# A fixed order from the output projection on, and the first down tile moved into the first pool

## The chip, the cores and the metric

The kernel runs on one core of one Trainium2 chip. The metric is device time in microseconds (us), the median of several executions; the profile shows one further execution in detail. Five engines work side by side, each on its own queue and in the order of that queue: TensorE (PE; its weight loads are shown apart as PEld), VectorE (DVE), ScalarE (ACT), GpSimd (POOL) and SyncE (SP), which here issues all loads and stores. Engines wait for each other through semaphores.

## The reference

One decoder layer on 256 tokens of width 2048, in float32:

```
h   = RMSNorm(x);  p = h @ W_in
A   = sliding-window attention on one part of p;  R = gated linear recurrence on the rest
m   = concat[RMSNorm(A), R] @ W_out
x   = x + RMSNorm_post(m)
x   = x + RMSNorm_post2( relu(RMSNorm_pre2(x) @ W_up)^2 @ W_down )
```

W_out is 2048 x 2048, W_up 2048 x 8192, W_down 8192 x 2048. The change lies between the last quarter of `@ W_out` and the first quarter of `@ W_down`.

## The kernel before, in words

Every float32 product is made of three fast products. A weight tile of 128 x 4 x 512 (1 MB) is loaded raw; ScalarE casts it to a rounded high part (`whi`), VectorE subtracts that from the raw tile to get the low part (`wlo`), and activations are split in the same way. TensorE then multiplies high by high, high activation by low weight, and low activation by high weight, adding all three in one PSUM bank (`three`, lines 109 to 113, for the steps here; `product`, line 785, later on).

Tokens come in two blocks of 128 (`tb` 0 and 1). The output projection runs in four column blocks of 512; the last one goes block by block of tokens, so that the work after it can begin on tb 0. That work is: scale by the post norm and add to x (`residual`), sum the squares of the new x (`norm2`), scale by the second norm (`hn`), and turn the result by transposes on TensorE into `h2T` (`turn`: four transposes into a PSUM bank of the tag `sc`, a copy by ScalarE for the high part, a subtraction by VectorE for the low part). The first two column blocks of W_up are made as plain products from `h2T`: block 0 one token block after the other, block 1 in alternation. After them a loop over segments covers the rest of W_up by sums of activations and weights with fewer products (the sums `s1` to `s4` are turned like `hn`), mixed with the segments of W_down. A segment is one weight tile and its matmuls; the loop prepares the tile of segment k+2 (cast and subtraction) while segment k is multiplied.

Weights live in two pools. The first, `wpool_a`, has three raw buffers and four each of `whi` and `wlo`. The second, `wpool_c`, opens after up block 1, in the same memory, with buffers X, P, Q and d (two each) and three each of `whi` and `wlo`. PSUM has three banks of the tag `sc`; a down column holds two of them from its first half to its second.

What sets the order: TensorE follows the program text from line 660 on (`order_pe`). On VectorE, ScalarE and SyncE a scheduler chooses the order until line 1013, where `order_all` fixes these too.

Of the kernel before, what the change touches and what calls it, by code (L numbers as in the profile page):

```python
# [29 lines left out]
def tile_hybrid_layer(  # L30
# [149 lines left out]
    def small(shape, tag, bufs=2):  # L180
        return cpool.tile([P] + list(shape), F32, tag=tag, name=nm(tag), bufs=bufs)
# [453 lines left out]
    def norm2(tb):  # L635
        s2 = small([4], f"s2{tb}")
        for c in range(4):
            square(x2[tb][:, c * 512:(c + 1) * 512], s2[:, c:c + 1])
        st = small([1], "st")
        nc.vector.reduce_sum(out=st, in_=s2, axis=AX.X)  # L640
        nc.vector.tensor_scalar(out=st, in0=st, scalar1=EPS, scalar2=None, op0=ALU.add)
        nc.gpsimd.tensor_tensor(out=rh[:, tb:tb + 1], in0=st, in1=mhalf[:, 0:1], op=ALU.pow)
        for c in range(4):
            cs = slice(c * 512, (c + 1) * 512)
            nc.vector.scalar_tensor_tensor(out=hn[tb][:, cs], in0=x2[tb][:, cs], scalar=rh[:, tb:tb + 1], in1=gpre[c],
                                           op0=ALU.mult, op1=ALU.mult)

    for c in range(3):
        ch = load_wide(w_out_v, 0, c * 512)
# [29 lines left out]
    def new_uT(first="mu0", second="mu1"):  # L679
        return [hpool.tile([P, 4, 2, S], F32R, tag=t, name=nm("uT")) for t in (first, second)]  # L680

    ch = load_wide(w_out_v, 0, 3 * 512, pieces=2)
    banks = [bank("pj"), bank("pj")]
    for kt in range(NKT):
        wide_step(banks[0], ch, mixT, 0, kt)
    evac_post(3, 0, banks[0])
    residual(0)
    norm2(0)
    up_w = load_wide(w_up_v, 0, 0, pieces=2)
    for kt in range(NKT):  # L690
        if kt in (9, 11, 13, 15):
            turn(0, (kt - 9) // 2)
        wide_step(banks[1], ch, mixT, 1, kt)
    evac_post(3, 1, banks[1])
    residual(1)
    norm2(1)


    uT = new_uT()
    ps = [bank("pj"), bank("pj")]  # L700
    for kt in range(NKT):
        if kt in (12, 13, 14, 15):
            turn(1, kt - 12)
        wide_step(ps[0], up_w, h2T, 0, kt)
    u = [new_u(), new_u()]
    relu(u[0], ps[0])
    for kt in range(NKT):
        if kt == 4:
            turn_u(uT, 0, 0, u[0], "tr", 1)
        wide_step(ps[1], up_w, h2T, 1, kt)  # L710
    relu(u[1], ps[1])

# [29 lines left out]
    in_h2T("a22", 1, 1)  # L742
    in_h2T("s4", 1, 0)

    up_w = load_wide(w_up_v, 0, 512)
    nc.vector.tensor_sub(out=tmp, in0=half(1, 0), in1=half(1, 1))
    nc.vector.tensor_sub(out=half(1, 0), in0=half(0, 0), in1=half(1, 0))
    ps = [bank("pj"), bank("pj")]
    for i in range(4):
        for tb in range(2):  # L750
            if i == 0 and tb == 1:
                turn_u(uT, 0, 1, u[1], "tr", 1)
            if i == 1:
                turn_sum(("s1", tmp), tb)
                if tb == 1:
                    nc.vector.tensor_sub(out=tmp, in0=tmp, in1=half(0, 0))
                    nc.vector.tensor_add(out=half(0, 0), in0=half(0, 1), in1=tmp)
            if i == 2:
                turn_sum(("s3", half(1, 0)), tb)
            if i == 3:  # L760
                turn_sum(("s2", tmp), tb)
            for j in range(4):
                wide_step(ps[tb], up_w, h2T, tb, 4 * i + j)
    prev = {}
    for tb in range(2):
        u = new_u()
        relu(u, ps[tb])
        prev[1, tb] = u

    pb.__exit__(None, None, None)  # L770
    pool_w.__exit__(None, None, None)
    wp[0] = ctx.enter_context(tc.tile_pool(name="wpool_c", bufs=2, side="right", reuse_waits="tile"))

    def raw_tile(tag, wv, kt0, c0):
        t = wp[0].tile([P, 4, 512], F32, tag=tag, name=nm(tag), bufs=2)
# [124 lines left out]
    def period(ch, m1_next):  # L900
# [40 lines left out]
        for k, to, frm, c, h in plan:  # L941
            q[k].adds.append(plus(to, frm, c, h))
        if ch == 1:
            q[0].turns += [lambda c=c: turn_sum(("s4", half(0, 0)), c) for c in range(2)]
            q[1].turns.append(t(d, 1, 0, d))
            q[2].turns.append(t(d, 1, 1, d))
            loads = [(0, "d", d, 1, 0), (1, "d", d, 1, 1), (4, "d", d, 2, 0), (7, "d", d, 2, 1),
                     (8, "R", ch, 0), (9, "R", ch, 1), (10, "d", d, 3, 0), (11, "Q", nx, 0), (12, "Q", nx, 1),
                     (13, "d", d, 3, 1), (14, "X", nx, 0), (15, "X", nx, 1), (16, "P", nx, 0), (17, "P", nx, 1),
                     (19, "d", ch, 0, 0), (21, "d", ch, 0, 1)]  # L950
# [62 lines left out]
    order_all = tc.manual_schedule(engines={mybir.EngineType.DVE, mybir.EngineType.Activation, mybir.EngineType.SP})  # L1013
    order_all.__enter__()
    load_down(0, 0, 0)
    for h in range(2):
        load_up("X", 1, h)
    load_down(0, 0, 1)
    for h in range(2):
# [53 lines left out]
```

## Time and profile before

| | us |
|---|---|
| median of 3 runs | 1118.68 (1118.08 to 1118.79) |
| the profiled execution | 1118.42 |
| its span, first to last instruction | 1116.7 |
| TensorE busy in the span | 1086.6 (97%) |
| VectorE busy | 846.1 (76%) |
| ScalarE busy | 623.1 (56%) |

The span is what the views below cut up; 1.7 us of the execution lie around it. TensorE is busy nearly always, so the views that matter are those that show where it is not: its own order in time with the idle time before each instruction and what ended it, and the clock that it was granted.

### The profile page before, as it was taken

How to read it: one execution, taken by the hardware profiler on the slowest of the kernel's cores; microseconds unless marked ns; L12 is line 12 of the kernel's file. 1: busy time of each engine (PE TensorE's matmuls, PEld its weight loads, DVE VectorE, ACT ScalarE, POOL GpSimd, SP SyncE). 2: the span in 40 equal slices, each digit the busy share in tenths (PEclk: the TensorE clock that was granted, in tenths of full speed). 3: DMA queues.
4: the chain of work that ended last, by engine and by line, in shares of the span. 5: the costliest groups of instructions: out<-in, count | busy, mean ns of one | idle time of the engine just before them, and what ended most of it. 6: DMA issues, size and time to landing. Idle time of an engine off the chain costs nothing.

```text
span 1116.7 us, 14041 instructions
## 1 busy us (share of the span) xinstructions
PE 1086.6 (97%) x5708; PEld 926.3 (83%) x5708; DVE 846.1 (76%) x765; ACT 623.1 (56%) x719; POOL 19.8 (2%) x48
## 2 busy tenths in 40 slices
PE   8999989999999989899999999999999999999996
PEld 7999889999988867778788888888888888888885
DVE  6755666665655557498998898898898898898565
ACT  6554565545454445455675575575575575575542
POOL 2100000000000000000000000000000000000000
PEclk9999989999999989999999999999999999999999
DMA  8743424444458645726728638638638638534662
GB/s 270 246 164 115 151 76 152 151 151 151 152 190 311 215 158 183 263 83 222 259 92 284 227 99 281 223 103 279 220 108 277 218 112 277 214 114 151 236 253 76
DMA packets 125538, 209.61 MB, mean 188 GB/s; under 512 B 3945, under 2 KB 49570, under 8 KB 124450
## 3 DMA queue, kind: packets, MB, share of 16 engines
q1 hardware_dynamic: 125474, 208.72, 54.7%
q8 instruction: 45, 0.74, 0.3%
q14 instruction: 19, 0.16, 0.0%
HBM read 204.51 MB, written 4.19 MB: 187 GB/s over the span
## 4 chain that ended last, share of the span: by engine, by line
PE 89%; DVE 4%; ACT 2%; issue 1%; DMA 1%; POOL 0%; DVEq 0%; POOLq 0%; ACTq 0%
PE pj L785 21%; PE pj L112 10%; PE pj L113 10%; PE pj L111 10%; PE sc L112 8%; PE sc L111 8%; PE sc L113 8%; DVE wlo L91 2%; PE o L112 1%; PE o L113 1%; PE tr L112 1%; PE tr L113 1%; PE tr L111 1%; PE o L111 1%; ACT whi L90 1%
## 5 line engine op out<-in xcount | busy, mean ns | idle before, releaser
L91 DVE TENSOR_TENSOR wlo<-raw,whi 128x2048 fp32r<-128x2048 f32 (+2 forms) x84 | 152.8, 1832 | 74.6 <-ACT whi L90 74.3
L90 ACT CAST whi<-d 128x2048 fp32r<-128x2048 f32 x60 | 114.8, 1913 | 120.5 <-PE sc L113 85.9
L91 DVE TENSOR_TENSOR wlo<-d,whi 128x2048 fp32r<-128x2048 f32 x60 | 137.4, 2290 | 55.3 <-ACT whi L90 55.2
L90 ACT CAST whi<-raw 128x2048 fp32r<-128x2048 f32 (+2 forms) x84 | 127.8, 1539 | 77.4 <-PE pj L113 38.3
L112 PE MATMUL sc<-wlo,uT 128*128 128x512 f32 x384 | 150.5, 392 | 2.5 <-DVE wlo L91 2.5
L111 PE MATMUL sc<-whi,uT 128*128 128x512 f32 x384 | 150.5, 392 | 2.2 <-ACT whi L90 1.6
L113 PE MATMUL sc<-whi,uT 128*128 128x512 f32 x384 | 150.3, 391 | 0.4 <-DVE uT L677 0.4
L90 ACT CAST whi<-X 128x2048 fp32r<-128x2048 f32 x56 | 107.1, 1915 | 77.9 <-DVE X L789 32.3
L785 PE MATMUL pj<-whi,hT 128*128 128x512 f32 x448 | 143.9, 390 | 0.0
L91 DVE TENSOR_TENSOR wlo<-X,whi 128x2048 fp32r<-128x2048 f32 x56 | 127.9, 2286 | 2.5 <-ACT whi L90 2.5
L111 PE MATMUL pj<-hT,whi 128*128 128x256 f32 x384 | 110.5, 288 | 1.1 <-ACT whi L90 0.7
L113 PE MATMUL pj<-hT,wlo 128*128 128x256 f32 x384 | 110.5, 288 | 0.9 <-DVE wlo L91 0.8
L112 PE MATMUL pj<-hT,whi 128*128 128x256 f32 x384 | 111.2, 290 | 0.0
L785 PE MATMUL pj<-whi,a 128*128 128x512 f32 x336 | 109.9, 395 | 0.0
L785 PEld LDWEIGHTS pj<-whi,hT 128*128 128x128 f32 x448 | 84.1, 188 | 17.4
L112 PEld LDWEIGHTS sc<-wlo,uT 128*128 128x128 f32 x384 | 72.5, 189 | 18.3 <-DVE wlo L91 3.4
L111 PEld LDWEIGHTS sc<-whi,uT 128*128 128x128 f32 x384 | 72.4, 189 | 18.0 <-ACT whi L90 1.8
L785 PE MATMUL pj<-wlo,hT 128*128 128x512 f32 x224 | 87.2, 390 | 0.0
L113 PEld LDWEIGHTS sc<-whi,uT 128*128 128x128 f32 x384 | 72.5, 189 | 15.8 <-DVE uT L677 0.8
L91 DVE TENSOR_TENSOR wlo<-P,whi 128x2048 fp32r<-128x2048 f32 x32 | 73.2, 2291 | 13.8 <-ACT whi L90 13.8
L111 PE MATMUL pj<-whi,hT 128*128 128x512 f32 x192 | 76.0, 398 | 0.0
L111 PEld LDWEIGHTS pj<-hT,whi 128*128 128x128 f32 x384 | 74.1, 193 | 2.0 <-ACT whi L90 0.9
(262 smaller groups left out, 2041.6 us busy)
## 6 DMA issues: line engine op xcount, KB each, us to landing
d<-in_w_down_dram SPq DMA_DIRECT2D x60, 1024.0 KB, 5.0
P<-in_w_up_dram SPq DMA_DIRECT2D x28, 1024.0 KB, 5.5
raw<-in_w_in_dram SPq DMA_DIRECT2D x24, 1024.0 KB, 5.1
raw<-in_w_in_dram SPq DMA_DIRECT2D x35, 512.0 KB, 4.6
raw<-in_w_out_dram SPq DMA_DIRECT2D x16, 1024.0 KB, 5.0
X<-in_w_up_dram SPq DMA_DIRECT2D x14, 1024.0 KB, 5.5
Q<-in_w_up_dram SPq DMA_DIRECT2D x14, 1024.0 KB, 5.4
raw<-in_w_up_dram SPq DMA_DIRECT2D x8, 1024.0 KB, 5.5
```

The costliest lines, as they stand in the source:

```text
L90: nc.scalar.copy(out=hi[:, k], in_=raw[:, k])
L91: nc.vector.tensor_tensor(out=lo[:, k], in0=raw[:, k], in1=hi[:, k].bitcast(F32), op=ALU.subtract)
L111: nc.tensor.matmul(o, lhsT=ah, rhs=bh, start=first, stop=False)
L112: nc.tensor.matmul(o, lhsT=ah, rhs=bl, start=False, stop=False)
L113: nc.tensor.matmul(o, lhsT=al, rhs=bh, start=False, stop=last)
L785: nc.tensor.matmul(o, lhsT=a, rhs=b, start=fresh and kt == 0 and i == 0, stop=kt == 7 and i == 2, skip_group_check=not fresh)
```

## The change

The fixed order now begins right after TensorE's first half of the last output column, so that VectorE, ScalarE and SyncE follow the text from there. `norm2` is gone: the squares are taken inside `residual`, right behind each quarter of x, and the scaling is split in quarters that stand among the turns. Up block 0 is no longer made step by step but in parts: for each weight tile all high-by-high products (`hh`), all with the low activation (`lh`), and last all with the low weight (`hl`), so that a low weight part is needed late. A raw tile is loaded when the third tile before it has been split (`load_t(i + 3)`), and the cast and the subtraction are written out in halves at their places. Up block 1 takes its tiles (4 to 7) from the same chain. The first tile of W_down (`raw00`, `w00`) is now loaded and split in the first pool and multiplied before the second pool opens; the segment loop then begins with the first product of `X`, and the two turns of the sum `s4`, which stood before that down tile, stand behind it. One `whi` buffer of the second pool is taken by a tile that nothing uses.

```
     def residual(tb):
         r = rsq_part(pss[tb][:, 3:4], ppart[:, tb:tb + 1])
+        s2 = small([4], f"s2{tb}")
         for c in range(4):
             cs = slice(c * 512, (c + 1) * 512)
             nc.vector.scalar_tensor_tensor(out=x2[tb][:, cs], in0=acc[tb][:, cs], scalar=r, in1=x2[tb][:, cs],
                                            op0=ALU.mult, op1=ALU.add)
+            square(x2[tb][:, cs], s2[:, c:c + 1])
...
+    def lo_t(i, h):
+        k = slice(2 * h, 2 * h + 2)
+        hi, lo = up_w[i]
+        nc.vector.tensor_tensor(out=lo[:, k], in0=up_raw[i][:, k], in1=hi[:, k].bitcast(F32), op=ALU.subtract)
+        if h == 1:
+            load_t(i + 3)
...
+    def part(tb, tile, kind):
+        for kt in range(4 * tile, 4 * tile + 4):
+            a = tok(h2T, kt, tb)[1 if kind == "lh" else 0]
+            b = up_w[tile][1 if kind == "hl" else 0][:, kt % 4, :]
+            nc.tensor.matmul(ps[tb], lhsT=a, rhs=b, start=kt == 0 and kind == "hh", stop=kt == NKT - 1 and kind == "hl")
...
-    for kt in range(NKT):
-        if kt in (9, 11, 13, 15):
-            turn(0, (kt - 9) // 2)
-        wide_step(banks[1], ch, mixT, 1, kt)
+    order_all.__enter__()
     evac_post(3, 0, banks[0])
+    residual(0)()
...
+    w3(0, 11)
+    scaled(0, 0)
+    scaled(0, 1)
+    cast2(0)
+    turn(0, 0)
+    scaled(0, 2)
+    w3(11, 13)
+    turn(0, 1)
+    cast2(1)
+    scaled(0, 3)
+    lo_t(0, 0)
+    w3(13, 15)
+    turn(0, 2)
+    w3(15, 16)
+    turn(0, 3)
     evac_post(3, 1, banks[1])
+    lo_t(0, 1)
+    cast2(2)
...
+    for tile_ in (0, 1):
+        part(0, tile_, "hh")
+    for tile_ in (0, 1):
+        part(0, tile_, "lh")
+    residual(1)()
+    part(0, 2, "hh")
+    part(0, 2, "lh")
+    cast2(3)
+    scaled(1, 0)
+    scaled(1, 1)
+    part(0, 0, "hl")
+    part(0, 3, "hh")
+    turn(1, 0)
...
+    turn(1, 3)
+    lo2(1)
+    part(1, 2, "hh")
+    part(1, 3, "hh")
+    for tile_ in range(4):
+        part(1, tile_, "lh")
+    lo2(2)
+    lo2(3)
+    part(1, 0, "hl")
+    for tile_ in range(1, 4):
+        for tb in range(2):
+            part(tb, tile_, "hl")
...
+    down_half(0, 0, 0, uT, w00, evac=False)
+    pb.__exit__(None, None, None)
+    pool_w.__exit__(None, None, None)
+    wp[0] = ctx.enter_context(tc.tile_pool(name="wpool_c", bufs=2, side="right", reuse_waits="tile"))
...
-            q = [dn[0][0], m1_first[0], m1_first[1], dn[0][1], m5[0], m5[1], dn[1][0], m6[0], m6[1], dn[1][1],
+            q = [None, m1_first[0], m1_first[1], dn[0][1], m5[0], m5[1], dn[1][0], m6[0], m6[1], dn[1][1],
...
-            q[0].turns += [lambda c=c: turn_sum(("s4", half(0, 0)), c) for c in range(2)]
+            q[1].turns += [lambda c=c: turn_sum(("s4", half(0, 0)), c) for c in range(2)]
...
+    wp[0].tile([P, 4, 512], F32R, tag="whi", name="unused", bufs=3)
     prepare(0, lambda: [load_up("Q", 1, h) for h in range(2)])
+    relu_first(0)
     prepare(1)
+    relu_first(1)
```

TensorE where the second pool opens, before: the turns of `s4` (from `hn`), then the first down tile (`whi_4344`, `wlo_4349`).

```order
L113 MATMUL pj_4167<-whi_4160,hT_3355 128x512
L627 MATMUL sc_4360<-ident,hn_3840 128x128 [waits DVE_49]
L627 MATMUL sc_4360<-ident,hn_3840 128x128 x3
L627 MATMUL sc_4367<-ident,hn_3840 128x128 [waits DVE_49]
L627 MATMUL sc_4367<-ident,hn_3840 128x128 x3
L111 MATMUL sc_4374<-whi_4344,uT_3995 128x512 [waits DVE_49,Activation_49]
L112 MATMUL sc_4374<-wlo_4349,uT_3995 128x512 [waits DVE_49]
```

The same place on TensorE now: the end of the first down tile (`whi_4271`, `wlo_4272`, banks `sc_4328` and `sc_4329`), then the turns of `s4`, then the first turn of up block 1 (`u_4381`).

```order
L112 MATMUL sc_4329<-wlo_4272,uT_3961 128x512
L113 MATMUL sc_4329<-whi_4271,uT_3961 128x512
L637 MATMUL sc_4394<-ident,hn_3857 128x128 [waits DVE_49]
L637 MATMUL sc_4394<-ident,hn_3857 128x128 x3
L637 MATMUL sc_4401<-ident,hn_3857 128x128 [waits DVE_49]
L637 MATMUL sc_4401<-ident,hn_3857 128x128 x3
L669 MATMUL sc_4408<-ident,u_4381 128x128 [waits DVE_49]
```

The down tile has moved ahead of the turns; its two banks stay taken, and the three turns behind it pass one after the other through the third bank of the tag.

VectorE at that place, before: the low parts of the first three segments, then the low parts of the turned `s4` (`hT_3352`, `hT_3353`).

```order
L91 TENSOR_TENSOR wlo_4349<-d_4332,whi_4344 128x2048 [waits DMAHW3_49,PE_49,Activation_49]
L91 TENSOR_TENSOR wlo_4353<-X_4334,whi_4352 128x2048 [waits DMAHW4_49,Activation_49]
L91 TENSOR_TENSOR wlo_4357<-X_4336,whi_4356 128x2048 [waits DMAHW5_49,Activation_49]
L630 TENSOR_TENSOR hT_3352<-sc_4360,hT_3352 128x4x128 [waits Activation_49]
L630 TENSOR_TENSOR hT_3353<-sc_4367,hT_3353 128x4x128 [waits Activation_49]
```

And now, from the low part of the first down tile (`wlo_4272`) on:

```order
L91 TENSOR_TENSOR wlo_4272<-raw_4150,whi_4271 128x2048 [waits DMAHW3_49,Activation_49]
L640 TENSOR_TENSOR a_4135<-sc_4287,a_4135 128x4x128 [waits Activation_49]
L640 TENSOR_TENSOR a_4135<-sc_4306,a_4135 128x4x128 [waits Activation_49]
L91 TENSOR_TENSOR wlo_4378<-X_4360,whi_4373 128x2048 [waits DMAHW4_49,Activation_49]
L91 TENSOR_TENSOR wlo_4384<-X_4362,whi_4383 128x2048 [waits DMAHW5_49,Activation_49]
L873 TENSOR_TENSOR X_4360<-X_4360,P_4368 128x2048 [waits DMAHW0_49,DVE_49]
L91 TENSOR_TENSOR wlo_4391<-d_4364,whi_4390 128x2048 [waits DMAHW6_49,Activation_49]
L640 TENSOR_TENSOR hT_3352<-sc_4394,hT_3352 128x4x128 [waits Activation_49]
L640 TENSOR_TENSOR hT_3353<-sc_4401,hT_3353 128x4x128 [waits Activation_49]
```

Four operations of 128 x 2048 now stand between the last low part of the first pool and the first low part of `s4`.

ScalarE at that place, before and then now: the casts of the first three segments.

```order
L90 CAST whi_4344<-d_4332 128x2048 [waits DMAHW3_49,DVE_49]
L90 CAST whi_4352<-X_4334 128x2048 [waits DMAHW4_49,DVE_49]
L90 CAST whi_4356<-X_4336 128x2048 [waits DMAHW5_49,DVE_49]
L629 CAST hT_3352<-sc_4360 128x4x128 [waits PE_49]
L629 CAST hT_3353<-sc_4367 128x4x128 [waits PE_49]
```

```order
L90 CAST whi_4373<-X_4360 128x2048 [waits DMAHW4_49,DVE_49,PE_49]
L664 ACTIVATE u_4381<-pj_4153 128x512
L90 CAST whi_4383<-X_4362 128x2048 [waits DMAHW5_49]
L664 ACTIVATE u_4387<-pj_4154 128x512
L90 CAST whi_4390<-d_4364 128x2048 [waits DMAHW6_49]
L639 CAST hT_3352<-sc_4394 128x4x128 [waits PE_49]
```

The first cast of the segment loop now has a wait for TensorE (PE_49) that it did not have before; in the built program `whi_4373` has the address of `whi_4271`, and the matmul that the wait names is the last one of the first down tile.

## Rows read from the trace of the kernel before

**Rows 1.** The page: its first line and TensorE's share.

```profile
span 1116.7 us, 14041 instructions
PE 1086.6 (97%) x5708; PEld 926.3 (83%) x5708; DVE 846.1 (76%) x765; ACT 623.1 (56%) x719; POOL 19.8 (2%) x48
```

**Rows 2.** TensorE in time: start us, us, engine, line, operation [idle before <-releaser].

```profile
402.20 0.39 PE L113 MATMUL pj<-whi,mu 128*128 128x512 f32 x1
408.13 1.12 PE L627 MATMUL sc<-ident,hn 128*128 128x128 f32 x4 [5.54 <-DVE hn L645]
...
413.83 0.60 PE L627 MATMUL sc<-ident,hn 128*128 128x128 f32 x4
...
415.65 0.60 PE L627 MATMUL sc<-ident,hn 128*128 128x128 f32 x4
...
427.24 0.63 PE L627 MATMUL sc<-ident,hn 128*128 128x128 f32 x4 [2.12 <-DVE hn L645]
...
470.95 0.50 PE L111 MATMUL sc<-whi,uT 128*128 128x512 f32 x1 [1.60 <-ACT whi L90]
473.27 0.50 PE L112 MATMUL sc<-wlo,uT 128*128 128x512 f32 x1 [1.82 <-DVE wlo L91]
...
478.28 0.50 PE L111 MATMUL sc<-whi,uT 128*128 128x512 f32 x1 [0.64 <-DVE hT L630]
...
491.25 0.50 PE L113 MATMUL sc<-whi,uT 128*128 128x512 f32 x1 [0.36 <-DVE uT L677]
...
500.19 0.50 PE L112 MATMUL sc<-wlo,uT 128*128 128x512 f32 x1 [0.66 <-DVE wlo L91]
```

**Rows 3.** The chain that ended last: start us, us, what.

```profile
505.74 5.44 PE pj L785 x24
```

**Rows 4.** Windows of 2 us: busy time of each engine, granted clock, DMA share, GB/s.

```profile
406.00:408.00 2.00, 0.00 (x0) 0.00 (x0) 1.30 (x5) 0.00 (x0) 0.55 (x1) 0.50 0.97 309
426.00:428.00 2.00, 0.76 (x6) 0.75 (x7) 1.65 (x3) 0.09 (x1) 0.31 (x1) 1.00 0.93 381
474.00:476.00 2.00, 2.00 (x7) 1.51 (x6) 2.00 (x2) 1.47 (x3) 0.00 (x0) 0.50 0.80 216
```

**Rows 5.** VectorE in time, residual and norm of token block 0.

```profile
398.70 2.74 DVE L618 SCALAR_TENSOR_TENSOR x<-mg,rf,x 128x512 f32<-128x512 f32 x4 [0.66 <-POOL rf L600]
...
404.04 2.36 DVE L91 TENSOR_TENSOR wlo<-raw,whi 128x1024 fp32r<-128x1024 f32 x2 [0.33 <-ACT whi L90]
406.32 0.15 DVE L640 TENSOR_REDUCE st<-s 128x1 f32<-128x4 f32 x1
```

**Rows 6.** ScalarE in time: the last square with its sum, and casts.

```profile
404.86 0.62 ACT L589 ACTIVATE junk<-x 128x512 f32<-128x512 f32 x1
405.39 0.18 ACT L589 ACTIVATION_READ_ACCUMULATOR junk<-x 128x1 f32 x1
...
413.34 2.00 ACT L90 CAST whi<-raw 128x1024 fp32r<-128x1024 f32 x2
...
470.79 3.70 ACT L90 CAST whi<-X 128x2048 fp32r<-128x2048 f32 x2
```

**Rows 7.** The page, DMA issues: KB each, median us from issue to landing.

```profile
raw<-in_w_up_dram SPq DMA_DIRECT2D x8, 1024.0 KB, 5.5
```

**Rows 8.** One turn in time, through TensorE, ScalarE and VectorE.

```profile
449.10 0.60 PE L627 MATMUL sc<-ident,tmp 128*128 128x128 f32 x4
...
449.73 0.59 ACT L629 CAST a<-sc 128x512 fp32r<-128x512 f32 x1 [1.95 <-PE sc L627]
...
450.35 0.69 DVE L630 TENSOR_TENSOR a<-sc,a 128x512 fp32r<-128x512 f32 x1 [0.90 <-ACT a L629]
```

**Rows 9.** VectorE in time, three operations of 128 x 2048 on end.

```profile
500.05 2.29 DVE L91 TENSOR_TENSOR wlo<-X,whi 128x2048 fp32r<-128x2048 f32 x1
502.25 2.29 DVE L789 TENSOR_TENSOR P<-P,Q 128x2048 f32<-128x2048 f32 x1
504.45 2.29 DVE L91 TENSOR_TENSOR wlo<-X,whi 128x2048 fp32r<-128x2048 f32 x1
```

More of the change, by code (lines that the diff above doesn't have):

```diff
@@ L619, in residual, with stats @@
                                            op0=ALU.mult, op1=ALU.add)
+            square(x2[tb][:, cs], s2[:, c:c + 1])
         nc.sync.dma_start(out=x2_dram[tb], in_=x2[tb])
         hn[tb] = keep.tile([P, D], F32, tag=f"acc{tb}", name=nm("hn"))
+        def stats():
+            st = small([1], "st")
+            nc.vector.reduce_sum(out=st, in_=s2, axis=AX.X)
+            nc.vector.tensor_scalar(out=st, in0=st, scalar1=EPS, scalar2=None, op0=ALU.add)
+            nc.gpsimd.tensor_tensor(out=rh[:, tb:tb + 1], in0=st, in1=mhalf[:, 0:1], op=ALU.pow)
+        return stats
     def turn_act(src, hi, lo, tag="sc", bufs=3):
@@ L633, in turn @@
         turn_act(hn[tb][:, c * 512:(c + 1) * 512], *(h2T[c][:, :, i, tb * P:(tb + 1) * P] for i in range(2)))
[L635 to L646, printed above, removed]
     for c in range(3):
@@ L680, in new_uT, with load_t, cast_t, split_t @@
         return [hpool.tile([P, 4, 2, S], F32R, tag=t, name=nm("uT")) for t in (first, second)]
+    up_raw, up_w = {}, {}
+    def load_t(i):
+        if i < 8:
+            up_raw[i] = load_raw(w_up_v[:, 4 * (i % 4):4 * (i % 4) + 4, (i // 4) * 512:(i // 4 + 1) * 512])
+    def cast_t(i, h):
+        if h == 0:
+            up_w[i] = [wp[0].tile([P, 4, 512], F32R, tag=t, name=nm(t), bufs=4) for t in ("whi", "wlo")]
+        k = slice(2 * h, 2 * h + 2)
+        nc.scalar.copy(out=up_w[i][0][:, k], in_=up_raw[i][:, k])
+    def lo_t(i, h):
+        k = slice(2 * h, 2 * h + 2)
+        hi, lo = up_w[i]
+        nc.vector.tensor_tensor(out=lo[:, k], in0=up_raw[i][:, k], in1=hi[:, k].bitcast(F32), op=ALU.subtract)
+        if h == 1:
+            load_t(i + 3)
+    def split_t(i):
+        up_w[i] = split_weight(None, up_raw[i])
+        load_t(i + 3)
+    def scaled(tb, c):
+        cs = slice(c * 512, (c + 1) * 512)
+        nc.vector.scalar_tensor_tensor(out=hn[tb][:, cs], in0=x2[tb][:, cs], scalar=rh[:, tb:tb + 1], in1=gpre[c],
+                                       op0=ALU.mult, op1=ALU.mult)
     ch = load_wide(w_out_v, 0, 3 * 512, pieces=2)
@@ L685, in tile_hybrid_layer @@
         wide_step(banks[0], ch, mixT, 0, kt)
+    for i in range(3):
+        load_t(i)
+    order_all = tc.manual_schedule(engines={mybir.EngineType.DVE, mybir.EngineType.Activation, mybir.EngineType.SP})
+    order_all.__enter__()
     evac_post(3, 0, banks[0])
-    residual(0)
-    norm2(0)
-    up_w = load_wide(w_up_v, 0, 0, pieces=2)
-    for kt in range(NKT):
-        if kt in (9, 11, 13, 15):
-            turn(0, (kt - 9) // 2)
-        wide_step(banks[1], ch, mixT, 1, kt)
+    residual(0)()
@@ new lines, in w3, with cast2 @@
+    def w3(a, b):
+        for kt in range(a, b):
+            wide_step(banks[1], ch, mixT, 1, kt)
+    ps = []
+    def part(tb, tile, kind):
[3 more added lines that the diff above has]
+            nc.tensor.matmul(ps[tb], lhsT=a, rhs=b, start=kt == 0 and kind == "hh", stop=kt == NKT - 1 and kind == "hl")
+    def cast2(i):
+        cast_t(i, 0)
+        cast_t(i, 1)
@@ L694, in tile_hybrid_layer, with lo2 @@
+    def lo2(i):
+        lo_t(i, 0)
+        lo_t(i, 1)
+    w3(0, 11)
[13 more added lines that the diff above has]
+    turn(0, 3)
     evac_post(3, 1, banks[1])
-    residual(1)
-    norm2(1)
+    lo_t(0, 1)
+    cast2(2)
     uT = new_uT()
[L700 to L704, printed above, removed]
@@ L705, in tile_hybrid_layer @@
-    u = [new_u(), new_u()]
[L706 to L711, printed above, removed]
+    ps += [bank("pj"), bank("pj")]
+    for tile_ in (0, 1):
[10 more added lines that the diff above has]
+    part(0, 3, "hh")
@@ L715, in half @@
+    turn(1, 0)
+    part(0, 3, "lh")
+    scaled(1, 2)
+    turn(1, 1)
+    part(1, 0, "hh")
+    scaled(1, 3)
+    turn(1, 2)
+    part(1, 1, "hh")
+    turn(1, 3)
[10 more added lines that the diff above has]
+            part(tb, tile_, "hl")
+    u = [new_u(), new_u()]
     def half(tb, h):
@@ L743, in tile_hybrid_layer @@
     in_h2T("s4", 1, 0)
-    up_w = load_wide(w_up_v, 0, 512)
     nc.vector.tensor_sub(out=tmp, in0=half(1, 0), in1=half(1, 1))
     nc.vector.tensor_sub(out=half(1, 0), in0=half(0, 0), in1=half(1, 0))
+    split_t(4)
+    relu(u[0], ps[0])
+    split_t(5)
+    raw00 = load_raw(w_down_v[:, 0:4, 0:512])
+    relu(u[1], ps[1])
     ps = [bank("pj"), bank("pj")]
@@ L751, in tile_hybrid_layer @@
             if i == 0 and tb == 1:
+                turn_u(uT, 0, 0, u[0], "tr", 1)
+                split_t(6)
+            if i == 2 and tb == 0:
                 turn_u(uT, 0, 1, u[1], "tr", 1)
@@ L756, in tile_hybrid_layer @@
                     nc.vector.tensor_sub(out=tmp, in0=tmp, in1=half(0, 0))
+                    split_t(7)
                     nc.vector.tensor_add(out=half(0, 0), in0=half(0, 1), in1=tmp)
@@ L761, in tile_hybrid_layer @@
                 turn_sum(("s2", tmp), tb)
+            if i == 2 and tb == 1:
+                w00 = split_weight(None, raw00)
             for j in range(4):
-                wide_step(ps[tb], up_w, h2T, tb, 4 * i + j)
+                wide_step(ps[tb], [up_w[4 + k] for k in range(i + 1)], h2T, tb, 4 * i + j)
     prev = {}
[L765 to L772, printed above, removed]
     def raw_tile(tag, wv, kt0, c0):
@@ L839, in down_half, with relu_first @@
                 evac_down(ch, c, tb, banks[tb])
+    def relu_first(tb):
+        prev[1, tb] = new_u()
+        relu(prev[1, tb], ps[tb])
+    down_half(0, 0, 0, uT, w00, evac=False)
+    pb.__exit__(None, None, None)
+    pool_w.__exit__(None, None, None)
+    wp[0] = ctx.enter_context(tc.tile_pool(name="wpool_c", bufs=2, side="right", reuse_waits="tile"))
     class Seg:
@@ L943, in period @@
         if ch == 1:
-            q[0].turns += [lambda c=c: turn_sum(("s4", half(0, 0)), c) for c in range(2)]
+            q[1].turns += [lambda c=c: turn_sum(("s4", half(0, 0)), c) for c in range(2)]
             q[1].turns.append(t(d, 1, 0, d))
             q[2].turns.append(t(d, 1, 1, d))
-            loads = [(0, "d", d, 1, 0), (1, "d", d, 1, 1), (4, "d", d, 2, 0), (7, "d", d, 2, 1),
+            loads = [(1, "d", d, 1, 1), (4, "d", d, 2, 0), (7, "d", d, 2, 1),
                      (8, "R", ch, 0), (9, "R", ch, 1), (10, "d", d, 3, 0), (11, "Q", nx, 0), (12, "Q", nx, 1),
@@ L1011, in tile_hybrid_layer @@
     segs += end + [Seg(lambda h=h: raws["d", last, 3, h], None) for h in range(2)]
[L1013 to L1017, printed above, removed]
+    load_up("X", 1, 0)
+    load_up("X", 1, 1)
     load_down(0, 0, 1)
+    load_down(0, 1, 0)
     for h in range(2):
```

## The prediction

> **What bounds the kernel now.** The page comes first. TensorE is busy for 1086.6 of 1116.7 us [rows 1], so no other engine's length matters by itself: time is won or lost only where TensorE stands or runs slowly. Next comes TensorE in time with the idle time in brackets, for the stretch that the change rewrites, 402 to 500 us. The reader is to see seven places where it loses time [rows 2]. A few corrections make the brackets into losses. In the segment loop 24 matmuls take 5.44 us, 0.227 each [rows 3], while a row shows 0.39 for one; a bracket is counted from that end, so a wait costs 0.16 more than its bracket. One turn and six matmuls take 1.82 us (413.83 to 415.65), so a turn alone takes 0.46.
>
> First place: after 402.20 TensorE is free at 402.43, waits until 408.13 for the scaled `hn`, and at 413.83 has done only two groups of turn and six matmuls, 3.64 us of work. The loss is 413.83 - 402.43 - 3.64 = 7.8 us. Of this 5.7 is the wait and 2.1 the clock: the granted clock is 0.50 of full, the level of 1.2 GHz, in the window 406 to 408 [rows 4]. Second: 2.12 + 0.16 = 2.3 at 427.24, with the clock at 1.00 there. Third and fourth, at the opening of the second pool: 1.6 for the cast, then 1.82 + 0.27 = 2.1 for the low part (the row before it has 0.50). Fifth: from 473.27 to 478.28 there are 11 matmuls, 2.5 us at the full rate, in 5.0: 2.5 lost, partly at a clock of 0.50 [rows 4]. Sixth and seventh: 0.5 and 0.8. All told 7.8 + 2.3 + 1.6 + 2.1 + 2.5 + 0.5 + 0.8 = 17.6 us. That is all that a better order can win here; the matmuls and turns themselves stay the same in number.
>
> **The change part by part.** I build up what TensorE loses in the same stretch afterwards.
>
> A, the first turn. The four updates of x still end at 398.70 + 2.74 = 401.44 [rows 5]. The last square then follows at once, since no cast stands before it: 0.71 us (404.86 to 405.57) [rows 6], to 402.2. From the sum of the squares to the turn took 408.13 - 406.32 = 1.81 [rows 2, 5], so the turn starts at 404.0. TensorE has two more steps before it than it had, six matmuls, and is free at 402.43 + 1.36 = 403.8. Loss 0.2 in place of 7.8.
>
> B, weight tile 3. Its load is queued behind the second half of tile 0's low part, which stands on VectorE behind the evacuation of the output projection. From 404.0: two groups of 1.82, then turn, three matmuls and the last turn; that turn starts at 408.8 and TensorE is free at 409.3. Copy (0.60 + 0.59 behind the turn's start) [rows 8], square 0.71, product about 0.6, half a low part 1.18 (2.36 for two) [rows 5]: 412.6. The load takes 5.5 [rows 7], half a cast 1.0 [rows 6]: 419.2. TensorE has 28 matmuls until then, 6.35 us, free at 415.6. It waits 3.5, does two matmuls, and waits another 0.5 for the second half of the cast. Loss 4.0; this takes the place of the second wait of 2.3.
>
> C, weight tile 4 for up block 1, loaded behind the low parts of tile 1. From the start of the last turn of token block 1: 1.95 for the turn through VectorE [rows 8], 2.36 for two halves, 5.5 for the load, 1.85 for the cast [rows 6], 2.29 for the low part [rows 9]: 13.95. TensorE has the turn, 52 matmuls of parts and one of block 1: 0.46 + 12.0 = 12.5. Loss 1.5.
>
> D, the opening of the second pool. The first cast of the segment loop has a new wait for the last matmul of the moved down tile, whose high part lay in that memory. Behind it on ScalarE stand the next two casts and the copy of the first `s4` turn, on VectorE everything: low part, low part, sum of X and P, low part, and only then the low part of that turn. The second `s4` turn needs the bank that this releases, as both other banks of the tag hold the down tile's results. So from the last matmul's end: cast 1.85, four operations 2.20 apart [rows 9] make 8.8, the turn's low part 0.69, handoffs about 0.15: 11.5. Add 0.16 as for every wait, take off the 0.46 of the first `s4` turn, which TensorE does meanwhile: loss 11.2. ScalarE is no later: its three casts and two short activations end before VectorE's third operation does.
>
> E, the turn behind it, again through the third bank: 1.95 from turn to low part [rows 8] less 0.46: loss 1.5.
>
> F, the clock. A wait of 5.5 us was followed by 2.1 us of slow running, and the pair of 1.60 and 1.82 by 2.5 - 0.64 - 0.16 = 1.7. Eleven microseconds are not in the trace. The bounds are 1.7 and twice 2.1, if the wait in E prolongs it; I take 2.1, as after the longest wait seen.
>
> The remaining waits of before (0.5 and 0.8) were VectorE just behind TensorE; after D, TensorE begins with the low parts of three segments ready, so they go. Sum: 0.2 + 4.0 + 1.5 + 11.2 + 1.5 + 2.1 = 20.5 against 17.6, a loss of 2.9 us.
>
> What I cost at nothing: the squares inside `residual`, the split scaling and the cast halves lie beside TensorE's matmuls but for A and B. The store of x on SyncE's queue for block 1 stands before the load of tile 4, which waits for VectorE far longer. The loads of X and d now stand behind those of tile 7 and the down tile; they are issued when tiles 4 and 5 have been split, over 20 us before D, and land in 5.5. P for the sum waits for the down tile's low part, 24 down matmuls (5.4 us) and more before D; if it were late, D would grow by as much.
>
> The profiled execution took 1118.42 us; with 2.9 it is 1121.3. The median of the runs is 0.26 above that execution, so I predict 1121.6 us.
>
> **The rivals.** First, the other side: D does not happen, because the cast need not wait for the down tile. ScalarE would be free after the last turn of up block 1, 36 matmuls (8.2 us) less a copy of about 1.2 before D begins, and everything behind it would start 7.0 earlier: D is 4.2, and the clock term perhaps 0. The time is then 1118.7 + 2.9 - 7.0 - 2.1 to 0, about 1112.5 to 1114.6. It would already be faster than before by more than can be told if D were under 6. Against it: the wait stands in ScalarE's queue in the built program, and the addresses are the same. For it: a tile is taken and not used just there, so the place in memory had some purpose.
>
> Second, the clock pays more often. The wait of 3.5 in B lies between one that did not lower the clock (2.1) and one that did (5.5); with another 2.1 there, and D's slow stretch twice as long, the loss is 2.9 + 2.1 to 2.9 + 4.2: 1123.7 to 1125.8. The Trainium skill (TensorE: Matmul & The Clock Gate, section Part 1: The HAM clock gate) says that the gate judges activity over a window that runs freely and is not started by the kernel. By that rule the wait in B would cost 2.1 in some executions and nothing in others; no row here shows a wait of that size, so the trace leaves it open.
>
> Third, no change to be told: loads land sooner and VectorE's operations start earlier than I have them, so that B is 3.0, C 0.6 and F 1.7. The loss is then 2.9 - 1.0 - 0.9 - 0.4 = 0.6: 1119.3.
>
> **How the numbers follow.** The forecast has 0.52, the second rival 0.24, the third 0.14, the first 0.10. What a measurement can tell from no change is 0.2%, 2.2 us here: above 1120.9 or below 1116.4. The forecast's own range is 1120.6 to 1123.6 (B and C half a microsecond shorter each; F at its upper bound); a tenth of it lies below 1120.9 and goes to "same". So slower 0.47 + 0.24 + 0.03 = 0.74, same 0.05 + 0.11 = 0.16, faster 0.10. The range from 1119.0 to 1125.0 leaves out the first rival and the ends of the others.
>
> **What would show it.** A: the first turn of `hn` at about 404 with almost no wait. B: a wait of 3 to 4 us before the `hh` products of tile 3, ended by the cast. C: one to two for the low part of tile 4. D: a wait of about 11 us before the second `s4` turn, ended by VectorE, with the first cast of the loop starting only when the down tile's last matmul has ended; the granted clock near 0.5 behind it. If the cast of X starts while the down tile is multiplied, D is wrong and the kernel is faster. If VectorE's queue there holds another order or the turn finds a free bank, likewise.

## The result, and the profile after

The changed kernel takes 1123.56 us (median of 5 runs, 1122.47 to 1125.39) where the kernel before takes 1118.79 in the same session: a ratio of 1.0045, 95% interval 1.0034 to 1.0057. It is slower, by about 4.8 us; 2.9 were forecast. The execution that the profile shows took 1124.23, 0.7 above the median. Its page:

```profile
span 1122.5 us, 14032 instructions
...
PE 1088.4 (97%) x5708; PEld 928.5 (83%) x5708; DVE 846.4 (75%) x765; ACT 623.0 (55%) x719; POOL 19.1 (2%) x48
```

The span is 5.8 us longer than in [rows 1]. TensorE has the same 5708 instructions, so again only its waits and its clock matter. TensorE in time, the places that answer to [rows 2]:

```profile
404.26 0.66 PE L637 MATMUL sc<-ident,hn 128*128 128x128 f32 x4 [0.18 <-DVE hn L704]
...
419.53 0.73 PE L730 MATMUL pj<-whi,hT 128*128 128x512 f32 x2 [3.46 <-ACT whi L689]
420.48 1.22 PE L730 MATMUL pj<-whi,hT 128*128 128x512 f32 x2 [0.22 <-ACT whi L689]
...
426.59 0.63 PE L637 MATMUL sc<-ident,hn 128*128 128x128 f32 x4
...
440.60 0.50 PE L112 MATMUL pj<-wlo,hT 128*128 128x512 f32 x1 [1.27 <-DVE wlo L91]
...
471.50 0.60 PE L637 MATMUL sc<-ident,hn 128*128 128x128 f32 x4
483.26 1.12 PE L637 MATMUL sc<-ident,hn 128*128 128x128 f32 x4 [11.16 <-DVE hT L640]
485.77 1.11 PE L669 MATMUL sc<-ident,u 128*128 128x128 f32 x4 [1.40 <-DVE hT L640]
...
495.02 0.39 PE L111 MATMUL sc<-whi,uT 128*128 128x512 f32 x1
```

The wait of 5.54 before the first turn has shrunk to 0.18 and that of 2.12 is gone. In their place stand 3.46 and 0.22 for the cast of weight tile 3, 1.27 for the low part of tile 4, and, between the two `s4` turns, 11.16; the turn behind them waits 1.40. (The last row is the first matmul of the next down tile; it waits for nothing.) Loads stand in the chain that ended last, just ahead of the first two of these places (start, us, what):

```profile
412.88 5.54 DMA raw<-in_w_up_dram
430.90 5.33 DMA raw<-in_w_up_dram
```

The first starts as VectorE has done the half low part that frees its buffer (411.60 + 1.22 = 412.82), and the cast starts as it has landed (412.88 + 5.54 = 418.42); VectorE's and ScalarE's rows:

```profile
411.60 1.22 DVE L694 TENSOR_TENSOR wlo<-raw,whi 128x1024 fp32r<-128x1024 f32 x1
```

```profile
418.44 1.99 ACT L689 CAST whi<-raw 128x1024 fp32r<-128x1024 f32 x2 [1.34 <-DMA raw<-in_w_up_dram]
```

Now the 11 us. ScalarE in time:

```profile
471.69 1.90 ACT L90 CAST whi<-X 128x2048 fp32r<-128x2048 f32 x1 [7.61 <-PE sc L113]
...
473.99 1.89 ACT L90 CAST whi<-X 128x2048 fp32r<-128x2048 f32 x1
...
476.26 1.90 ACT L90 CAST whi<-d 128x2048 fp32r<-128x2048 f32 x1
478.05 0.59 ACT L639 CAST hT<-sc 128x512 fp32r<-128x512 f32 x1
```

And VectorE:

```profile
473.62 4.57 DVE L91 TENSOR_TENSOR wlo<-X,whi 128x2048 fp32r<-128x2048 f32 x2 [8.82 <-ACT whi L90]
478.12 2.28 DVE L873 TENSOR_TENSOR X<-X,P 128x2048 f32<-128x2048 f32 x1
480.32 2.28 DVE L91 TENSOR_TENSOR wlo<-d,whi 128x2048 fp32r<-128x2048 f32 x1
482.52 0.68 DVE L640 TENSOR_TENSOR hT<-sc,hT 128x512 fp32r<-128x512 f32 x1
```

ScalarE stands for 7.61 us until the last matmul of the down tile (`sc`, line 113) releases its cast. VectorE has four operations on end before the one that frees the bank, and TensorE starts again 0.06 us after that one ends (482.52 + 0.68 = 483.20). The clock, in windows of 2 us (columns as in [rows 4]):

```profile
420.00:422.00 2.00, 1.78 (x7) 1.22 (x6) 0.00 (x0) 0.43 (x1) 0.00 (x0) 0.54 0.01 4
422.00:424.00 2.00, 2.00 (x9) 1.64 (x8) 0.79 (x2) 0.59 (x1) 0.00 (x0) 0.61 0.00 0
...
484.00:486.00 2.00, 0.60 (x3) 0.23 (x2) 0.69 (x1) 0.59 (x1) 0.00 (x0) 0.50 0.93 309
490.00:492.00 2.00, 2.00 (x7) 1.41 (x7) 1.10 (x1) 0.00 (x0) 0.00 (x0) 0.54 0.00 0
492.00:494.00 2.00, 2.00 (x12) 1.69 (x11) 0.04 (x1) 1.98 (x2) 0.00 (x0) 1.00 0.00 0
```

So the clock was at half, the level of 1.2 GHz, behind the wait of 3.46 too, and behind that of 11.16 until almost 492. The chain shows what this does to 12 matmuls, before and after the clock came back:

```profile
486.89 5.10 PE pj L869 x12
492.42 2.76 PE pj L869 x12
```

### The profile page after: what moved, and what is told of

The parts are those of the page before. It is cut to its first block, busy times and chain, and to the rows that moved or that the text cites. A ratio compares the mean times of both kernels' runs of the same rounds, so it can differ in the third digit from the quotient of the medians.

```text
span 1122.5 us, 14032 instructions
## 1 busy us (share of the span) xinstructions
PE 1088.4 (97%) x5708; PEld 928.5 (83%) x5708; DVE 846.4 (75%) x765; ACT 623.0 (55%) x719; POOL 19.1 (2%) x48
## 4 chain that ended last, share of the span: by engine, by line
PE 90%; DVE 3%; DMA 3%; ACT 2%; issue 1%; SPq 0%; POOL 0%; DVEq 0%; POOLq 0%; ACTq 0%
PE pj L869 22%; PE pj L112 10%; PE pj L113 10%; PE pj L111 10%; PE sc L113 8%; PE sc L111 8%; PE sc L112 8%; DVE wlo L91 2%; PE o L112 1%; PE tr L113 1%; PE o L113 1%; PE tr L112 1%; PE tr L111 1%; ACT whi L90 1%; PE o L111 1%; PE sc L669 1%
## 5 line engine op out<-in xcount | busy, mean ns | idle before, releaser
L91 DVE TENSOR_TENSOR wlo<-raw,whi 128x2048 fp32r<-128x2048 f32 (+2 forms) x77 | 145.6, 1901 | 72.5 <-ACT whi L90 71.3
L91 DVE TENSOR_TENSOR wlo<-d,whi 128x2048 fp32r<-128x2048 f32 x59 | 135.1, 2289 | 49.2 <-ACT whi L90 49.2
L90 ACT CAST whi<-raw 128x2048 fp32r<-128x2048 f32 (+2 forms) x77 | 121.8, 1596 | 80.9 <-PE pj L113 33.2
L869 PE MATMUL pj<-whi,hT 128*128 128x512 f32 x448 | 145.7, 394 | 0.0
L113 PEld LDWEIGHTS pj<-hT,wlo 128*128 128x128 f32 x384 | 74.3, 193 | 0.8 <-DVE wlo L91 0.8
```

What stands on the lines that cost most here:

```text
L90: nc.scalar.copy(out=hi[:, k], in_=raw[:, k])
L91: nc.vector.tensor_tensor(out=lo[:, k], in0=raw[:, k], in1=hi[:, k].bitcast(F32), op=ALU.subtract)
L113: nc.tensor.matmul(o, lhsT=al, rhs=bh, start=False, stop=last)
L869: nc.tensor.matmul(o, lhsT=a, rhs=b, start=fresh and kt == 0 and i == 0, stop=kt == 7 and i == 2, skip_group_check=not fresh)
```

## The experiments

Theory: the loss is made in the opening of the second pool by two things together, the memory that the first cast waits for and the one free bank that the turns pass through, and it is made larger by the clock. Rivals: the first part loses (late loads, order by parts); or the clock alone does. All ratios are to the kernel before, with 95% intervals; a time is the median of a run's executions. A recorded ratio can differ from the quotient of the medians by up to 0.13% (e_both: 1111.40 against 1118.71), so a difference of a microsecond between two runs is not certain.

| run | us | ratio to the kernel before |
|---|---|---|
| the change | 1123.56 | 1.0045 (1.0034 to 1.0057) |
| e_down_back | 1114.56 | 0.9963 (0.9950 to 0.9975) |
| e_down_only | 1125.35 | 1.0059 (1.0047 to 1.0072) |
| e_s4 | 1116.48 | 0.9983 (0.9974 to 0.9992) |
| e_buf | 1116.99 | 0.9988 (0.9979 to 0.9997) |
| e_both | 1111.40 | 0.9948 (0.9935 to 0.9962) |
| e_clock | 1121.55 | 1.0032 (1.0019 to 1.0044) |
| e_clockb | 1121.43 | 1.0026 (1.0017 to 1.0036) |
| e_parts | 1129.55 | 1.0097 (1.0081 to 1.0112) |
| e_best | 1109.10 | 0.9911 (0.9896 to 0.9926) |
| e_warm | 1107.48 | 0.9903 (0.9887 to 0.9920) |

**The two parts of the change, each alone.** First the change without the moved down tile:

```
...
-    down_half(0, 0, 0, uT, w00, evac=False)
...
-            q = [None, m1_first[0], ...
+            q = [dn[0][0], m1_first[0], ...
...
-            q[1].turns += [lambda c=c: turn_sum(("s4", ...
+            q[0].turns += [lambda c=c: turn_sum(("s4", ...
...
+    load_down(0, 0, 0)
...
```

> The changed kernel with the first down tile put back behind the opening of the second pool, as the kernel before has it (with its load, its place in the segment loop and the s4 turns ahead of it); the fixed order and the products in parts stay. This is the first part of the change alone. Theory (the first part gains, the moved down tile loses it all and more): the first turn has almost no wait, the waits of about 3.5 and 1.4 for weight tiles 3 and 4 stay, the opening of the pool shows the waits of the kernel before (1 to 3 us each, about 5 in all) and not 11: 1113.0 to 1115.5. Rival (the first part is neutral, what the first turn wins the late loads lose): 1118 to 1119.5. Rival (the first part is what loses): above 1120.

Measured 1114.56: the first part alone makes the kernel faster. TensorE at the opening of the pool:

```profile
469.21 0.50 PE L112 MATMUL sc<-wlo,uT 128*128 128x512 f32 x1 [1.11 <-DVE wlo L91]
474.23 0.50 PE L111 MATMUL sc<-whi,uT 128*128 128x512 f32 x1 [2.21 <-DVE hT L640]
```

Then the kernel before with the moved tile and nothing else:

```
+    raw00 = load_raw(w_down_v[:, 0:4, 0:512])
...
+                w00 = split_weight(None, raw00)
...
+    down_half(0, 0, 0, uT, w00, evac=False)
...
-            q = [dn[0][0], m1_first[0], ...
+            q = [None, m1_first[0], ...
...
```

> The kernel before with the moved down tile alone: loaded and split in the first pool, multiplied before the second opens, s4 turns behind it; no fixed order, no products in parts before it. This is the second part of the change alone. Theory: the waits of 5.5 and 2.1 of the kernel before stay, those at the opening of the pool (7.5 us of loss) are replaced by 11.3 + 1.6 and a half-clock stretch worth about 3.6: 7 to 9 us slower than the kernel before, 1125.5 to 1128. Rival (the two parts work only together: with the scheduler free until the pool opens, the first cast comes earlier and the wait is not there): 1118 to 1120.

Measured 1125.35, just under the range. The long wait is there to a hundredth:

```profile
486.27 1.11 PE L627 MATMUL sc<-ident,hn 128*128 128x128 f32 x4 [11.17 <-DVE hT L630]
```

So the moved tile loses and the order ahead of it gains. The two ratios make -0.37% and +0.59%, in sum +0.22%, where the change has +0.45%. That is at the edge of what the intervals allow; whether the parts hinder each other by a microsecond or two stays open.

**The two causes of the long wait.** The turns back ahead of the down tile:

```
+    for c in range(2):
+        turn_sum(("s4", half(0, 0)), c)
     down_half(0, 0, 0, uT, w00, evac=False)
...
-            q[1].turns += [lambda c=c: turn_sum(("s4", half(0, 0)), c) for c in range(2)]
```

> The changed kernel with one thing put back: the two turns of the sum s4 stand ahead of the first down tile on TensorE again. Theory (the loss lies in the opening of the second pool: the first cast waits for the down tile's memory, and the s4 turns behind the tile pass through one bank): the 11.2 us wait before the second s4 turn goes, and the 1.4 behind it; what is left is the cast and low part of the first X tile behind the down tile (1.85 + 2.2, less one turn) and the waits that the kernel before had further on (about 0.4, 2.2 and 0.9), so 5 us come back in waits and 0 to 3 in the clock: 1116.0 to 1118.7. Rival (the loss comes from the first part: loads that hang on low parts, products in parts): within 1 us of 1123.6, the 5 us turning up as other waits. Rival (the clock alone): faster by no more than the half-clock stretch behind 483 us, some 3.5 us, with the waits themselves merely moved: about 1120.

Measured 1116.48. What is left at the place is a wait of 2.48 us, now for ScalarE, where the relu stands behind the cast that still waits for the down tile:

```profile
475.34 1.12 PE L669 MATMUL sc<-ident,u 128*128 128x128 f32 x4 [2.48 <-ACT u L664]
```

The other cause by itself, the order left as it is:

```
-    wp[0].tile([P, 4, 512], F32R, tag="whi", name="unused", bufs=3)
+    unused = wp[0].tile([P, 4, 512], F32R, tag="whi", name="unused", bufs=3)
+    nc.gpsimd.memset(unused[:, 0, 0:1].bitcast(F32), 0.0)
```

> The changed kernel, in which GpSimd writes one column of the high-part tile of the second pool that nothing used, so that the tile really takes its place: the first segment's high part then lies on other memory than the moved down tile's. The order of the work is the same. Theory: the first cast of the loop no longer waits for the down tile's last matmul; the cast of the third segment, which now lies there, does. Behind the last matmul stand one cast (1.85), one low part (2.2) and the low part of the turn (0.7) instead of four operations of 2.2: the wait before the second s4 turn falls from 11.2 to about 5, the 1.4 stays, the clock gives back up to 2: 1115.5 to 1117.5. Rival (the order of the queues and not the memory makes the wait: the cast would come just as late without the dependence): 1123.6, wait still 11. Rival (first part): within 1 us of 1123.6.

Measured 1116.99. Without an access the extra tile had taken no place in memory, so the `whi` buffer that the section on the change counts as taken was still free; with one, the first two casts run beside the down tile, and only the third waits, for the write into that place, which itself comes behind the down tile's last matmul. ScalarE, then TensorE:

```profile
464.58 1.91 ACT L90 CAST whi<-X 128x2048 fp32r<-128x2048 f32 x1
...
472.47 1.90 ACT L90 CAST whi<-d 128x2048 fp32r<-128x2048 f32 x1 [3.19 <-POOL unused L1117]
```

```profile
477.35 1.11 PE L637 MATMUL sc<-ident,hn 128*128 128x128 f32 x4 [4.64 <-DVE hT L640]
```

The bank's wait falls from 11.16 to 4.64 with the same order of the queues: 6.5 of it was the memory. Both edits together:

> The changed kernel with both edits: s4 turns ahead of the down tile, and the unused high-part tile made real by a write of one column. Theory: nothing is late behind the down tile any more; both waits (11.2 and 1.4) and the half-clock stretch behind them go, and the later waits of the kernel before (about 2.2 and 0.9) come back: 9.8 us less in waits, 2 to 3.6 in the clock: 1110.2 to 1112.0, faster than the kernel before by 6 to 8. Rival (first part): not faster than the kernel before, since the late loads remain. Rival (the two edits remove the same wait twice): no better than the better of the two alone, about 1116.

Measured 1111.40. TensorE's waits between 395 and 510 us (what waits, for what: us in total, times, longest us) hold neither `s4` nor the turn behind it, but one of the kernel before's kind in the loop (`uT`, 0.36 there [rows 2] and 2.0 here), as expected:

```profile
PE pj L730 <- ACT whi L689: 3.3, 1, 3.3
PE sc L113 <- DVE uT L674: 2.0, 1, 2.0
PE pj L112 <- DVE wlo L91: 1.5, 1, 1.5
```

**The clock.** In the changed kernel, TensorE is given idle work in its long wait:

```
...
+                dead = bank("tr", 1)
+                for k in range(46):
+                    nc.tensor.matmul(dead, lhsT=uT[0][:, 0, 0, 0:P], rhs=uT[0][:, k % 4]..., start=True, stop=True)
...
```

> The changed kernel, with 46 matmuls of 128 x 512 that nothing uses on TensorE between the two s4 turns, in a bank that is free there: TensorE works through the long wait instead of standing. 46 x 0.227 = 10.4 us, so the wait falls to about 0.8 without ending later. Theory (the clock is part of the loss: it is granted at half until about 491.9, and the 7.2 us of work between 483.3 and then would take 3.6): granted clock 1.00 throughout there, 1119.5 to 1121.0, though TensorE does 10 us more work. Rival (the wait alone is the loss, the clock term was the 2.1 of the forecast or less): 1121.5 or more. Rival (the extra matmuls slow VectorE or ScalarE by their traffic): 1123.6 or more.

Measured 1121.55, outside the theory's range and just inside that of the rival by which the clock costs no more than the forecast's 2.1: 2.0 us less than the change by the medians, though the intervals of the two ratios overlap. TensorE:

```profile
472.35 10.71 PE L1040 MATMUL tr<-uT 128*128 128x512 f32 x46
483.78 0.66 PE L637 MATMUL sc<-ident,hn 128*128 128x128 f32 x4 [0.73 <-DVE hT L640]
485.84 1.11 PE L669 MATMUL sc<-ident,u 128*128 128x128 f32 x4 [1.40 <-DVE hT L640]
```

```profile
486.00:488.00 2.00, 2.00 (x7) 1.74 (x8) 0.00 (x0) 0.98 (x2) 0.00 (x0) 0.50 0.78 304
```

The granted clock is 1.00 in every window from 474 to 484, but behind the 0.73 and 1.40 that remain it falls after all. I had expected 1.00 throughout; that failed. From the second `s4` turn to the next down tile TensorE takes 10.0 us (483.78 to 493.82) in place of 11.8. That is no proof of the clock's price: where the long wait was left standing the same stretch took 10.3 in e_clockb, shown next, and 10.5 in e_down_only (486.27 to 496.78). The same for the wait for weight tile 3, ahead of `part(0, 3, "hh")`, with 14 matmuls:

> The changed kernel with 14 matmuls of 128 x 512 that nothing uses (3.2 us) on TensorE just before the high-by-high products of weight tile 3, in a bank that is free: they fill the wait for that tile's cast. Theory (a wait of 3.5 us lowers the clock here, contrary to the forecast): the granted clock stays at 1.00 from 420 to 424, and the 3.4 us at half that the changed kernel has there give back 1.2 to 1.8: 1121.6 to 1122.4. Rival (the forecast: this wait does not lower the clock): within 0.4 of 1123.6.

Measured 1121.43. The wait is 0.43, the clock 1.00 from 420 to 426, and from the first matmul of tile 3 to the fourth turn TensorE takes 424.83 - 419.18 = 5.65 us, where the changed kernel takes 426.59 - 419.53 = 7.06 for the same instructions:

```profile
419.18 0.73 PE L730 MATMUL pj<-whi,hT 128*128 128x512 f32 x2 [0.43 <-ACT whi L689]
...
424.83 0.62 PE L637 MATMUL sc<-ident,hn 128*128 128x128 f32 x4
...
481.58 1.11 PE L637 MATMUL sc<-ident,hn 128*128 128x128 f32 x4 [11.17 <-DVE hT L640]
...
491.91 0.39 PE L111 MATMUL sc<-whi,uT 128*128 128x512 f32 x1
```

So 1.4 us of the loss there are the clock's. The long wait is unchanged, but the stretch behind it took 1.4 less too (10.3 in place of 11.8), with nothing changed there: in this execution the clock came back sooner (0.74 in the window from 486). So the 2.1 us between the medians need not all be tile 3's, and since the intervals just touch, the rows are surer than the times. The rival by which the clock alone loses falls with e_s4 and e_buf: they gained 7.1 and 6.6 us by the medians, more than all that the clock took (4.8, worked out below).

**The order by parts.** Up block 0 made step by step again, with the low weight parts moved on VectorE to where TensorE then needs them:

```
-    for tile_ in (0, 1):
-        part(0, tile_, "hh")
...
+    def step(tb, tile):
+        for kt in range(4 * tile, 4 * tile + 4):
+            wide_step(ps[tb], [up_w.get(i) for i in range(4)], h2T, tb, kt)
...
+    step(0, 0)
+    lo2(1)
...
```

> The changed kernel with up block 0 made step by step again, three products for each of the 16 steps, one token block after the other; the low parts of the weight tiles are placed on VectorE as early as TensorE then needs them. All else stays. Theory (the order by parts is what lets TensorE go on while VectorE is behind): low weight parts are wanted at once, so TensorE waits about 1.7 for that of tile 0, about 4 for that of tile 1 or 2, and 2 to 4 more before a turn of token block 1 and after it, some 9 to 10 us in place of 5; with the clock behind these waits 4 to 7 us slower than the changed kernel: 1127 to 1131. Rival (the order by parts moves nothing but the place where the same low parts are waited for): 1122.5 to 1125.

Measured 1129.55. TensorE waits for low weight parts at once:

```profile
412.85 0.50 PE L112 MATMUL pj<-wlo,hT 128*128 128x512 f32 x1 [1.25 <-DVE wlo L694]
420.90 0.80 PE L112 MATMUL pj<-wlo,hT 128*128 128x512 f32 x1 [3.66 <-DVE wlo L694]
428.97 0.63 PE L637 MATMUL sc<-ident,hn 128*128 128x128 f32 x4 [1.59 <-DVE hn L704]
432.13 0.79 PE L112 MATMUL pj<-wlo,hT 128*128 128x512 f32 x1 [2.29 <-DVE wlo L694]
```

These four make 8.8 us in place of 3.46 + 0.22 + 1.27 = 5.0. Between the two profiled spans lie 7.4 us (1129.9 and 1122.5; 6.0 between the medians); the rest fits the longer stretches below full clock, in the windows from 420 to 428 and 430 to 438 where the changed kernel has 420 to 424. The order by parts is worth its place: the intervals of the two ratios lie apart.

**A better version.** To both edits of e_both, two low parts are placed earlier:

```
     lo_t(0, 0)
+    lo_t(0, 1)
...
     scaled(1, 3)
+    lo2(1)
     turn(1, 2)
...
```

> The kernel with both edits at the opening of the second pool (1111.4), and the low parts of weight tiles 0 and 1 placed earlier on VectorE: the second half of tile 0's right behind the first, that of tile 1 before the low part of the third turn of token block 1. Tiles 3 and 4 are then loaded earlier. Theory (the waits of 3.3 and 1.5 there hang on when those low parts are done): the first falls to 1.5 to 2.3 and perhaps no longer lowers the clock, the second goes: 1106.0 to 1108.5. Rival (the loads themselves are the limit, as the queue or the memory is full): within 1 us of 1111.4. Rival (the turns of hn come later by the low parts put before them): about 1110, with a new wait before a turn.

Measured 1109.10, a little over the range. The wait for tile 3 falls to 2.00 and that for tile 4 is gone, so the loads hung on the low parts. The rival with the later turns wanted a new wait before a turn; the trace has none. But the clock still falls, there and at the next wait. TensorE, and a window behind each of the two waits:

```profile
418.58 0.73 PE L730 MATMUL pj<-whi,hT 128*128 128x512 f32 x2 [2.00 <-ACT whi L689]
...
481.85 0.79 PE L113 MATMUL sc<-whi,uT 128*128 128x512 f32 x1 [2.00 <-DVE uT L674]
```

```profile
420.00:422.00 2.00, 2.00 (x10) 1.62 (x9) 0.51 (x2) 0.59 (x1) 0.00 (x0) 0.60 0.00 0
...
482.00:484.00 2.00, 2.00 (x5) 1.61 (x6) 2.00 (x2) 0.00 (x0) 0.00 (x0) 0.50 0.00 0
```

Last, 7 idle matmuls in the first of these waits, by the edit of e_clockb:

> The best kernel so far (1109.1) with 7 matmuls of 128 x 512 that nothing uses (1.6 us) in the 2.0 us wait for weight tile 3. Theory (2.0 us of standing lower the clock there, 420 to 424, 3.4 us at half): the granted clock stays at 1.00 from 418 to 426 and 1.2 to 1.8 come back: 1107.3 to 1107.9. Rival (the clock falls for what TensorE did before and not for this wait): 1109 or more, still half there.

Measured 1107.48, the best time of this study, 1.0% under the kernel before. TensorE, and a window behind each of the two waits:

```profile
418.36 0.73 PE L730 MATMUL pj<-whi,hT 128*128 128x512 f32 x2 [0.41 <-ACT whi L689]
...
480.22 0.50 PE L113 MATMUL sc<-whi,uT 128*128 128x512 f32 x1 [1.99 <-DVE uT L674]
```

```profile
420.00:422.00 2.00, 2.00 (x15) 1.74 (x14) 0.87 (x2) 0.71 (x2) 0.00 (x0) 1.00 0.00 0
...
480.00:482.00 2.00, 1.78 (x8) 1.48 (x9) 2.00 (x2) 0.00 (x0) 0.00 (x0) 1.00 0.00 0
```

From tile 3 to the fourth turn TensorE takes 5.66 us (418.36 to 424.02) in place of 7.21 in e_best (418.58 to 425.79). The interval overlaps that of e_best, so the gain between these two is shown by the rows and the medians, not by the ratios.

## Why the prediction was right, and where a term was not

Slower was forecast and the time lies in the range, but at the upper end of the forecast's own (1120.6 to 1123.6; with F at its bound the sum is 1121.6 + 2.1 = 1123.7) and just under the second rival's. By the same correction of 0.16 per wait, the terms of the changed kernel are:

| term | forecast | trace |
|---|---|---|
| A, first turn | 0.2 | 0.18 + 0.16 = 0.3 |
| B, weight tile 3 | 4.0 | 3.46 + 0.22 + 0.32 = 4.0 |
| C, weight tile 4 | 1.5 | 1.27 + 0.16 = 1.4 |
| D, opening of the pool | 11.2 | 11.16 + 0.16 = 11.3 |
| E, the turn behind it | 1.5 | 1.40 + 0.16 = 1.6 |
| F, the clock | 2.1 | 1.4 + 3.4 = 4.8 |
| sum | 20.5 | 23.4 |

Against the 17.6 that the kernel before loses this makes 5.8, as the spans differ. A to E came out within 0.2 each. D rests on two premises, and both were tested: e_buf took 6.5 us from its wait by moving a tile in memory, e_s4 8.7 by moving the turns, and with both nothing of it was left. The second premise was tested less sharply: e_s4 takes the turns out of the bank and out of VectorE's queue at once, and neither a free bank nor another order on VectorE was tried alone.

The step that was mis-sized is F. Its 4.8 are worked out so: 1.4 behind B (e_clockb against the changed kernel, above); behind D, from 483.26 to 495.02 are 11.8 us, in which TensorE has three turns and 24 matmuls, 3 x 0.46 + 5.44 = 6.8 at the full rate, and the wait of E, 1.6: 3.4 are left. The forecast took 2.1 once, as after the longest wait of the kernel before. It gave nothing to the wait in B, though by its own reading the pair of 1.60 and 1.82 had cost 1.7. That is the miss that shows in every profile: of the runs that leave the wait in B as it is, six have it at 3.25 to 3.46 us, and the clock fell each time.

Behind D the size is one execution's. In three other profiles with the same waits (11.16 or 11.17, then 1.40) the stretch took 10.3 (e_clockb), 10.5 (e_down_only) and 11.2 us (e_parts, 491.23 to 502.45), so that 2.0, 2.1 and 2.8 are left. With 2.1 there and 1.4 behind B the sum is 22.1, a loss of 4.5, near the 4.8 of the medians. So the second rival was half the case: the clock did pay in B, though 1.4 and not 2.1; the profiled execution lies in that rival's range (1124.23 in 1123.7 to 1125.8), the median just under it. That the forecast's 2.1 behind D was too small for most executions is not shown. The first rival fell with the cast at 471.69 waiting for the down tile; the third with B and C at full size.

Whether the wait of E prolongs the slow stretch behind D is not shown. In e_clock the clock held to 484 and fell behind 0.73 and 1.40, so that such short waits can be enough.

## What to carry to other kernels

When work is moved from one memory pool to the end of the pool before it, ask what lies on its buffers next: the first tile of the new pool may get the very memory that the moved work reads last, and then the preparation that used to run beside it queues behind it. Ask also which banks the moved work keeps, since turns behind it then share what is left. And price a new wait of some microseconds with the clock behind it, here 2.0 to 3.4 us behind 11.2 and 1.4 or more behind 3.3 to 3.5, also where a shorter one in the trace was free.

## What had not been expected of the hardware

A wait of one length does not always cost the clock. In e_best and e_warm the same wait for `uT` in the same order of work is 2.00 and 1.99 us; behind the one the window from 482 shows 0.50, behind the other, from 480, 1.00. Before the change 2.12 was free [rows 2, 4], while in e_s4 2.48 (0.50 in the window from 476) and in e_best the first 2.00 were followed by half clock. Nor did a longer wait cost more here: behind 4.64 in e_buf the stretch of three turns and 24 matmuls took 11.7 us (477.35 to 489.07), as behind 11.16. And where the wait in B cost 1.4 to 1.6 us in five profiles, against e_clockb's 5.65 to the fourth turn, it cost 2.4 in e_both (418.13 to 426.21). The Trainium skill (TensorE: Matmul & The Clock Gate, section Part 1: The HAM clock gate) has the gate look at activity in windows that run freely and don't start with the kernel; these rows agree, without proving it. Which waits will cost, and how much, cannot then be read from one profile; only that they can.
